# The window mask of the local attention, added by VectorE instead of TensorE

## The chip, the cores and the metric

One NeuronCore of a Trainium2 chip runs the whole program; seven other cores are idle. The metric is the time of one execution on the device, in microseconds, lower is better. Engines are named as in the profile: PE is TensorE, PEld its weight loads, DVE is VectorE, ACT is ScalarE, POOL is GpSimd, and SP issues the DMA transfers.

## The reference

The program is a two-layer block of a generator. Each layer normalises 1024 latent and 256 context tokens, projects them into four groups of heads (A: latent attention, B: global attention, C: attention within a window, with a sink, D: a state space scan), and projects the four results back. The change lies in group C. Cut to what matters, C computes for four heads of width 64:

```
def window_sink_attention(q, k, v, k_ctx, v_ctx, sink, scale):
    ...   # k_band: for each block of 128 queries the key blocks before, at and after it
    s_loc = jnp.einsum('bnqhgd,bnkhd->bnhgqk', qb, k_band).astype(jnp.float32) * scale
    s_ctx = jnp.einsum('bnqhgd,bkhd->bnhgqk', qb, k_ctx).astype(jnp.float32) * scale
    ...
    valid = (jnp.abs(k_pos - q_pos) <= WINDOW) & (k_pos >= 0) & (k_pos < n)
    s_loc = jnp.where(valid[None, :, None, None], s_loc, -jnp.inf)
    ...
    p = jax.nn.softmax(jnp.concatenate([s_ctx, s_loc, sink_col], axis=-1), axis=-1).astype(v.dtype)
    ...
```

WINDOW is 128. So a query block sees its own key block whole, a triangle of the block before and a triangle of the block after.

## The kernel before

Tokens are handled in tiles of 128. Attention runs over six pairs of heads per layer, in the order B, B, A, A, C, C. For each pair the queries come in groups (`gi`): 512 latent tokens, the other 512, and in the first layer the 256 context tokens. One group of one pair is a unit here. A unit has two interleaved activities:

- `main` computes the unit itself. For each key block and both heads it forms transposed scores in PSUM (tile `ps_st`, tag S2, three buffers), ACT writes their exponentials into `P` (L1224), two blocks later PE multiplies `P` with the values (L1231, tile `ps_acc`), and POOL or DVE adds `P` into running sums `ac` (L1240, L1246).
- Between its blocks `main` calls `pieces`: the steps of `maxima` for a later unit. Each step forms plain scores in PSUM (tile `ps_s`, tag MX, three buffers; L1143) and DVE takes the maximum of each row (L1147, tile `mp`), which later enters the exponent as one more row of the queries. In the last two units of a layer the pieces also split the output weights into high and low parts on DVE (`wo_hi` L1521, `wo_lo` L1522).

`mask_r` holds five blocks of 128 columns. The first three are the window mask: a triangle of 0 and -1e30, a block of zeros, the other triangle. In group C a score tile of 128, 256 or 384 columns gets the part of these three blocks that belongs to it (`mo` is its offset). Before the change it is added by PE: one more matmul with an identity as the weights accumulates the mask into the same PSUM tile, at L1145 for the maxima and at L1222 for the transposed scores.

The program is written as a sequence, and a scheduler orders the instructions of each engine and hands out buffers; each engine then runs its own list strictly in order. `tm` is a ring of eight buffers of 512 columns for short-lived tiles; `bg` is a ring of six buffers of 1024 columns that `P`, the raw weights `wo_raw` and the tiles `yh` and `yl` of the output projection share.

Of the kernel before, what the change touches and what calls it, by code (L numbers as in the profile page):

```python
# [9 lines left out]
F32 = mybir.dt.float32  # L10
F32R = mybir.dt.float32r
AF = mybir.ActivationFunctionType
ALU = mybir.AluOpType
# [4 lines left out]
P = 128  # L18
# [39 lines left out]
def hybrid_block(ctx, tc, x, ctxt, c_t, w_fm, w_tm, w_mod, b_gate, p_col, p_row, w_qu, w_kvu, w_out,  # L58
                 fnw, consts, rope_tm, rope_fm, out, dbg=None):
    nc = tc.nc  # L60
    DEPTH = w_fm.shape[0]
    cp = ctx.enter_context(tc.tile_pool(name="cp", bufs=1))
# [4 lines left out]
    mm = nc.tensor.matmul  # L67
# [44 lines left out]
    def small(shape, name, tag, bufs=2, dt=F32):  # L112
        return tp.tile(shape, dt, tag=tag, bufs=bufs, name=name)

    def ring(tag, bufs, cols):
        def f(shape=(P, cols), dt=F32, name=tag):
            return tp.tile(list(shape), dt, tag=tag, bufs=bufs, name=name)
        return f

    tm, ac, bg = ring("tm", 8, 512), ring("ac", 3, 1024), ring("bg", 6, 1024)  # L120
# [3 lines left out]
    def ps(tag, name=None):  # L124
        return pp.tile([P, 512], F32, tag=tag, bufs=PS_BUFS[tag], name=name or f"ps_{tag}")
# [6 lines left out]
    def f32(ap):  # L132
        return ap.bitcast(F32)
# [6 lines left out]
    def const(shape):  # L140

        n = int(np.prod(shape[1:]))
        v = con[:, con_at[0]:con_at[0] + n]
        con_at[0] += n
        assert con_at[0] <= CON_W
        return v if len(shape) == 2 else v.rearrange("p (a b) -> p a b", a=shape[1])
# [3 lines left out]
    ident, tri_u, tri_l, ones = [base[:, i * P:(i + 1) * P] for i in range(4)]  # L150
    rtm, cs = const([P, 8, 96]), const([P, 8, 32])
    mask_f = bg(name="mask_f")
    nc.sync.dma_start(out=mask_f[:, 0:5 * P], in_=consts[:, 4 * P:])
    mask_r = cp.tile([P, 6 * P], F32R, name="mask_r")
    nc.vector.tensor_copy(mask_r[:, 0:5 * P], mask_f[:, 0:5 * P])
    nc.vector.tensor_copy(mask_r[:, 5 * P:6 * P], ident)
    ident_r = mask_r[:, 5 * P:6 * P]
    st_r = [mask_r[:, 3 * P:4 * P], mask_r[:, 4 * P:5 * P]]
    mhalf = const([P, 16])
    nc.vector.memset(mhalf, -0.5)  # L160
    nc.vector.memset(cs, 0.0)
# [874 lines left out]
    def attention(L, res, need_ctx, y, late):  # L1036
# [90 lines left out]
        def maxima(op, gi):  # L1127
            lo, n = GROUPS[gi]
            nt = n // P
            br, kd = op["br"], op["kd"]  # L1130
            km = kd if br == 0 else P
            npc = 1 if gi == 0 else (3 if br < 2 else 2)
            st = {}

            def scored(h, parts, dst):

                qh = op["q"][h][0]
                kh = op["k"][h][0] if br == 0 else op["k"][0][0]
                p = ps("MX", name="ps_s")
                w = parts[0][2]  # L1140
                for u, (t, k0, w, mo) in enumerate(parts):
                    o = p[:, u * w:(u + 1) * w]
                    mm(o, lhsT=qh(lo + t * P, P, 0, km), rhs=kh(k0, w, 0, km), start=True, stop=mo is None)  # L1143
                    if mo is not None:
                        mm(o, lhsT=ident_r, rhs=mask_r[:, mo:mo + w], start=False, stop=True)  # L1145
                nu = len(parts)
                nc.vector.tensor_reduce(out=dst, in_=p[:, :nu * w].rearrange("p (u k) -> p u k", u=nu), axis=AX.X, op=ALU.max)  # L1147

            def begin():
                st["mp"] = small([P, 2, 4, 3], "mp", "mp", 2)  # L1150

            def ctx_part(h, t2):
                scored(h, [(t2 + u, 0, NCTX, None) for u in range(2)], st["mp"][:, h, t2:t2 + 2, 0])

            def lat_part(h, t, c):
                if br < 2:
                    scored(h, [(t, NCTX + c * 512, 512, None)], st["mp"][:, h, t, 1 + c:2 + c])
                else:
                    i = lo // P + t
                    j0, j1 = max(2, i - 1), min(NTILE - 1, i + 1)  # L1160
                    scored(h, [(t, j0 * P, (j1 - j0 + 1) * P, (j0 - i + 1) * P)], st["mp"][:, h, t, 1:2])

            def end():
                mt = small([P, 8], "mt", "mt", 2)
                mv = mt[:, 0:2 * nt].rearrange("p (h t) -> p h t", h=2)
                nc.vector.tensor_reduce(out=mv, in_=st["mp"][:, :, 0:nt, 0:npc], axis=AX.X, op=ALU.max)
                if br == 2:
                    p0 = op["pair"] * 2
                    nc.vector.tensor_tensor(out=mv, in0=mv, in1=sink8[:, p0:p0 + 2].unsqueeze(2).to_broadcast([P, 2, nt]), op=ALU.max)
                pm = ps("TR", name="ps_m")  # L1170
                nc.tensor.transpose(pm[0:2 * nt, 0:P], mt[:, :2 * nt], ident)
                ng = tm((8, P), F32R, name="ng")
                nc.scalar.activation(out=ng[0:2 * nt, :], in_=pm[0:2 * nt, 0:P], func=AF.Copy, scale=-1.0)
                for h in range(2):
                    nc.sync.dma_start(out=f32(op["q"][h][1](lo, n, kd, kd + 1)), in_=f32(ng[h * nt:(h + 1) * nt, :]))

            r = [begin]
            for h in range(2):
                r += [lambda h=h, t=t: ctx_part(h, t) for t in range(0, nt, 2)]
                if gi > 0:  # L1180
                    r += [lambda h=h, t=t, c=c: lat_part(h, t, c) for t in range(nt) for c in range(2 if br < 2 else 1)]
            return r + [end]
# [14 lines left out]
        def main(op, gi, pieces, tail):  # L1197
            lo, n = GROUPS[gi]
# [6 lines left out]
            def scores(bi):  # L1205
                kb, c0, w, mo = blocks[bi]
                k = lambda tok, rows: tok.tile(kb, 0, rows)
                pts = bg((P, 2, 512), name="P")
                for h in range(2):
                    st = ps("S2", name="ps_st")[:, :w]  # L1210
                    q0, q1 = op["q"][h]
                    q = lambda tok, rows: tok(lo + c0, w, 0, rows)
                    if br == 0:
                        k0, k1 = op["k"][h]
                        mm(st, lhsT=k(k0, 96), rhs=q(q0, 96), start=True, stop=False)  # L1215
                        mm(st, lhsT=k(k1, 96), rhs=q(q0, 96), start=False, stop=False)
                        mm(st, lhsT=k(k0, 97), rhs=q(q1, 97), start=False, stop=True)  # L1217
                    else:
                        k0, k1 = op["k"][0]
                        mm(st, lhsT=k(k0, 128), rhs=q(q0, 128), start=True, stop=False)  # L1220
                        if mo is not None:
                            mm(st, lhsT=ident_r, rhs=mask_r[:, mo:mo + w], start=False, stop=False)  # L1222
                        mm(st, lhsT=k(k1, 65), rhs=q(q1, 65), start=False, stop=True)  # L1223
                    nc.scalar.activation(out=pts[:, h, :w], in_=st, func=AF.Exp, scale=op["scale"])  # L1224
                return pts

# [30 lines left out]
            for bi in range(len(blocks)):  # L1257
                pts = scores(bi)
                batch.append((bi, pts))
                add(bi, pts)  # L1260
                if len(batch) == BATCH or bi == len(blocks) - 1:
                    for _ in range(2 if len(tail) > 3 else 1):
                        if tail:
                            tail.pop(0)()
                    flush_values()
                    todo.extend(batch)
                    batch = []
                want = min(total, -(-total * (bi + 1) // max(1, len(blocks) - LEAD)))
                while done < want:
                    pieces[done]()  # L1270
                    done += 1
            if br == 2:
                for h in range(2):
# [3 lines left out]
                                         scale=HEAD_SCALE, bias=pr[64:65, PR_SINK + hd:PR_SINK + hd + 1])  # L1277
                    nc.vector.tensor_tensor(out=sums[0][64:65, h, :n], in0=sums[0][64:65, h, :n], in1=es[64:65, :n], op=ALU.add)
            o = tm(name="o")
# [51 lines left out]
        for i, (br, pair) in enumerate(pairs):  # L1331
            op = ops[br, pair]
# [286 lines left out]
```

## Time and profile before

| | |
|---|---|
| time, median of 3 runs | 1849.13 us (1848.83 to 1856.71) |
| the profiled execution | 1844.81 us, its span 1843.0 us |
| busy share of the span | PE 95%, PEld 72%, DVE 61%, POOL 43%, ACT 40% |
| chain that ended last | PE 75%, DVE 11%, DMA 4%, issue 3%, POOL 3%, ACT 2% |

The span is what the profile covers, the time what the device reports for that execution. A busy share is a mean over stages with different limits. The chain is the sequence of waits followed back from the last instruction; an engine's share of it is the time during which that engine's work was what everything later waited for. In the first layer group C runs from about 787 us to 879 us of the span, in the second from about 1668 us to 1749 us; some of C's first maxima are already taken during the last unit of group A.

### The profile page before, as it was taken

How to read it: one execution, taken by the hardware profiler on the slowest of the kernel's cores; microseconds unless marked ns; L12 is line 12 of the kernel's file. 1: busy time of each engine (PE TensorE's matmuls, PEld its weight loads, DVE VectorE, ACT ScalarE, POOL GpSimd, SP SyncE). 2: the span in 40 equal slices, each digit the busy share in tenths (PEclk: the TensorE clock that was granted, in tenths of full speed). 3: DMA queues.
4: the chain of work that ended last, by engine and by line, in shares of the span. 5: the costliest groups of instructions: out<-in, count | busy, mean ns of one | idle time of the engine just before them, and what ended most of it. 6: DMA issues, size and time to landing. Idle time of an engine off the chain costs nothing.

```text
span 1843.0 us, 27921 instructions
## 1 busy us (share of the span) xinstructions
PE 1752.4 (95%) x9658; PEld 1329.2 (72%) x9658; DVE 1131.8 (61%) x2290; ACT 744.3 (40%) x2060; POOL 783.3 (43%) x735
## 2 busy tenths in 40 slices
PE   6999999999999999998999989999999999999898
PEld 4667888889975556565787768888998555566576
DVE  6867864373466655447546777753744766645953
ACT  5332433332224545556323333343332445455631
POOL 2322552132327766656224134531332576665522
PEclk9999999999999999999999989999999999999999
DMA  9474323255684332224411524231668623220521
GB/s 312 148 229 134 122 100 119 86 189 178 192 221 117 84 105 74 59 62 128 151 58 40 164 90 148 87 120 70 215 195 249 163 75 88 56 65 12 179 85 58
DMA packets 130397, 231.54 MB, mean 126 GB/s; under 512 B 13784, under 2 KB 74560, under 8 KB 130256
## 3 DMA queue, kind: packets, MB, share of 16 engines
q1 hardware_dynamic: 130256, 229.75, 40.2%
q8 instruction: 77, 1.26, 0.3%
q14 instruction: 64, 0.52, 0.1%
HBM read 161.15 MB, written 68.44 MB: 125 GB/s over the span
## 4 chain that ended last, share of the span: by engine, by line
PE 75%; DVE 11%; DMA 4%; issue 3%; POOL 3%; ACT 2%; SPq 0%; POOLq 0%; DVEq 0%; ACTq 0%
PE ps_acc L1231 10%; PE ps_fm L128 7%; PE ps_fm L130 7%; PE ps_fm L129 7%; PE ps_s L1143 6%; PE ps_o L129 3%; PE ps_o L130 3%; PE ps_o L128 3%; PE ps_st L1220 3%; PE ps_st L1223 3%; PE ps_tm L128 2%; PE ps_tm L130 2%; PE ps_tm L129 2%; PE ps_st L1215 2%; PE ps_st L1217 2%
## 5 line engine op out<-in xcount | busy, mean ns | idle before, releaser
L1246 POOL TENSOR_TENSOR ac<-ac,P 128x512 f32<-128x512 f32 (+3 forms) x248 | 310.8, 1274 | 134.8 <-ACT P L1224 114.5
L1147 DVE TENSOR_REDUCE mp<-ps_s 128x1 f32<-128x512 f32 (+3 forms) x428 | 260.7, 658 | 167.7 <-PE ps_s L1143 154.5
L1224 ACT ACTIVATE P<-ps_st 128x512 f32<-128x512 f32 (+3 forms) x456 | 238.0, 555 | 263.5 <-PE ps_st L1223 102.9
L128 PE MATMUL ps_fm<-hh,wfm_hi 128*128 128x512 f32 x576 | 234.3, 407 | 3.2 <-DVE kb L658 1.9
L130 PE MATMUL ps_fm<-hl,wfm_hi 128*128 128x512 f32 x576 | 231.3, 402 | 1.5 <-POOL hl L403 0.7
L129 PE MATMUL ps_fm<-hh,wfm_lo 128*128 128x512 f32 x576 | 229.9, 399 | 0.0
L128 PE MATMUL ps_tm<-wtm_hi,hh 128*128 128x256 f32 x512 | 146.5, 286 | 0.8 <-ACT va L870 0.6
L129 PE MATMUL ps_tm<-wtm_hi,hl 128*128 128x256 f32 x512 | 145.5, 284 | 0.0
L130 PE MATMUL ps_tm<-wtm_lo,hh 128*128 128x256 f32 x512 | 145.3, 284 | 0.0
L130 PEld LDWEIGHTS ps_fm<-hl,wfm_hi 128*128 128x128 f32 x576 | 109.2, 190 | 27.2 <-POOL hl L403 3.3
L128 PEld LDWEIGHTS ps_fm<-hh,wfm_hi 128*128 128x128 f32 x576 | 109.5, 190 | 26.5 <-ACT hf L399 3.3
L129 PEld LDWEIGHTS ps_fm<-hh,wfm_lo 128*128 128x128 f32 x576 | 109.6, 190 | 19.4 <-issue 0.8
L1240 POOL TENSOR_TENSOR ac<-P 128x1024 f32<-128x1024 f32 (+1 forms) x30 | 65.4, 2180 | 136.7 <-ACT P L1224 133.9
L128 PE MATMUL ps_o<-wo_hi,yh 128*128 128x512 f32 x288 | 113.3, 395 | 2.7 <-ACT yh L1373 2.7
L129 PE MATMUL ps_o<-wo_hi,yl 128*128 128x512 f32 x288 | 113.4, 394 | 0.5 <-DVE yl L1374 0.4
L130 PE MATMUL ps_o<-wo_lo,yh 128*128 128x512 f32 x288 | 112.9, 392 | 0.0
L1231 PE MATMUL ps_acc<-P,vt 128*64 128x512 f32 (+3 forms) x416 | 104.3, 542 | 0.0
L128 PEld LDWEIGHTS ps_tm<-wtm_hi,hh 128*128 128x128 f32 x512 | 98.1, 192 | 3.1 <-issue 1.6
L130 PEld LDWEIGHTS ps_tm<-wtm_lo,hh 128*128 128x128 f32 x512 | 98.2, 192 | 0.7 <-issue 0.4
L129 PEld LDWEIGHTS ps_tm<-wtm_hi,hl 128*128 128x128 f32 x512 | 98.2, 192 | 0.5
L1400 POOL TENSOR_TENSOR xres<-xres,dl 128x512 f32<-128x512 f32 x32 | 41.3, 1290 | 105.5 <-DVE dl L1399 105.5
L1246 DVE TENSOR_TENSOR ac<-ac,P 128x512 f32<-128x512 f32 (+3 forms) x88 | 64.8, 736 | 29.1 <-ACT P L1224 17.6
(345 smaller groups left out, 4150.4 us busy)
## 6 DMA issues: line engine op xcount, KB each, us to landing
wfm_raw<-in_w_fm_dram SPq DMA_DIRECT2D x36, 512.0 KB
wm<-in_w_mod_dram SPq DMA_DIRECT2D x64, 256.0 KB
d_q<-qkhl SPq DMA_DIRECT2D x18, 512.0 KB
wm<-in_w_mod_dram SPq DMA_DIRECT2D x16, 512.0 KB
d_gate<-th SPq DMA_DIRECT2D x32, 256.0 KB
wtm_raw<-in_w_tm_dram SPq DMA_DIRECT2D x16, 512.0 KB
qq<-d_q SPq DMA_DIRECT2D x32, 256.0 KB
wo_raw<-in_w_out_dram SPq DMA_DIRECT2D x16, 512.0 KB
```

The costliest lines, as they stand in the source:

```text
L128: mm(o, lhsT=lh, rhs=rh, start=first, stop=False)
L129: mm(o, lhsT=ll, rhs=rh, start=False, stop=False)
L130: return mm(o, lhsT=lh, rhs=rl, start=False, stop=last)
L1143: mm(o, lhsT=qh(lo + t * P, P, 0, km), rhs=kh(k0, w, 0, km), start=True, stop=mo is None)
L1147: nc.vector.tensor_reduce(out=dst, in_=p[:, :nu * w].rearrange("p (u k) -> p u k", u=nu), axis=AX.X, op=ALU.max)
L1220: mm(st, lhsT=k(k0, 128), rhs=q(q0, 128), start=True, stop=False)
L1223: mm(st, lhsT=k(k1, 65), rhs=q(q1, 65), start=False, stop=True)
L1224: nc.scalar.activation(out=pts[:, h, :w], in_=st, func=AF.Exp, scale=op["scale"])
L1231: mm(acc[h * 64:h * 64 + 64, c0:c0 + w], lhsT=op["v"].tile(kb)[:, v0:v0 + 64], rhs=pts[:, h, :w], start=(bi == 0), stop=(bi == len(blocks) ...
L1240: nc.gpsimd.tensor_tensor(out=s[:, :, :n], in0=sums[0][:, :, :n], in1=pts[:, :, :n], op=ALU.add)
L1246: eng.tensor_tensor(out=s[:, h, c0:c0 + w], in0=s[:, h, c0:c0 + w], in1=pts[:, h, :w], op=ALU.add)
L1400: (nc.vector if t == ts[-1] else nc.gpsimd).tensor_tensor(out=xt.t[:, js], in0=xt.t[:, js], in1=d, op=ALU.add)
```

## The change

The two masking matmuls are gone, and with them the identity in `mask_r`. In `maxima` one DVE instruction adds the mask to the scores and takes their maximum; it writes the sum to a buffer of the `tm` ring that nobody reads (`mjunk`). In `main` a DVE addition in place, in PSUM, stands between the matmuls and the exponential; it covers the two triangles only, not the zero block between them: 128 columns for a tile of 128 or 256 columns, two blocks of 128 for a tile of 384.

```
-    mask_r = cp.tile([P, 6 * P], F32R, name="mask_r")
-    nc.vector.tensor_copy(mask_r[:, 0:5 * P], mask_f[:, 0:5 * P])
-    nc.vector.tensor_copy(mask_r[:, 5 * P:6 * P], ident)
-    ident_r = mask_r[:, 5 * P:6 * P]
+    mask_r = cp.tile([P, 5 * P], F32R, name="mask_r")
+    nc.vector.tensor_copy(mask_r, mask_f[:, 0:5 * P])
     st_r = [mask_r[:, 3 * P:4 * P], mask_r[:, 4 * P:5 * P]]
+    win = mask_r.bitcast(F32)
...
-                    mm(o, lhsT=qh(lo + t * P, P, 0, km), rhs=kh(k0, w, 0, km), start=True, stop=mo is None)
+                    mm(o, lhsT=qh(lo + t * P, P, 0, km), rhs=kh(k0, w, 0, km), start=True, stop=True)
                     if mo is not None:
-                        mm(o, lhsT=ident_r, rhs=mask_r[:, mo:mo + w], start=False, stop=True)
+                        junk = tm(name="mjunk")
+                        nc.vector.tensor_tensor_reduce(out=junk[:, :w], in0=o, in1=win[:, mo:mo + w], scale=1.0, scalar=-3e38,
+                                                       op0=ALU.add, op1=ALU.max, accum_out=dst)
+                        return
...
                         mm(st, lhsT=k(k0, 128), rhs=q(q0, 128), start=True, stop=False)
-                        if mo is not None:
-                            mm(st, lhsT=ident_r, rhs=mask_r[:, mo:mo + w], start=False, stop=False)
                         mm(st, lhsT=k(k1, 65), rhs=q(q1, 65), start=False, stop=True)
+                    if mo is not None:
+                        b0, b1 = mo // P, (mo + w) // P - 1
+                        blocks_of = lambda v, b: v.rearrange("p (b c) -> p b c", c=P)[:, b, :]
+                        outer = slice(0 if b0 == 0 else 2 - b0, (2 if b1 == 2 else 0) - b0 + 1, 2)
+                        v = blocks_of(st, outer)
+                        nc.vector.tensor_tensor(out=v, in0=v, in1=blocks_of(win[:, 0:3 * P], slice(outer.start + b0, outer.stop + b0, 2)),
+                                                op=ALU.add)
                     nc.scalar.activation(out=pts[:, h, :w], in_=st, func=AF.Exp, scale=op["scale"])
```

The first place is DVE's list in the second layer, in the second unit of group C. Before, from the addition of a `P` of 128 columns to that of one of 384:

```order
L1246 TENSOR_TENSOR ac<-ac,P 128x128
L1147 TENSOR_REDUCE mp<-ps_s 128x1 x2
L1147 TENSOR_REDUCE mp<-ps_s 128x2
L1301 RECIPROCAL asum<-asum 128x8
L1147 TENSOR_REDUCE mp<-ps_s 128x2
L1147 TENSOR_REDUCE mp<-ps_s 128x1 x2
L1246 TENSOR_TENSOR ac<-ac,P 128x384
```

After the change (lines from 1143 on have moved by some numbers; ISA is the new combined instruction, and `mp 128x1` the second instruction that it becomes, which reads out its maximum):

```order
L1145 ISA mjunk,mp<-ps_s,mask_r 128x384
L1145 ISA mp 128x1
L1149 TENSOR_REDUCE mp<-ps_s 128x2
L1229 TENSOR_TENSOR ps_st<-ps_st,mask_r 128x128 x2
L1149 TENSOR_REDUCE mp<-ps_s 128x2
L1145 ISA mjunk,mp<-ps_s,mask_r 128x256
L1145 ISA mp 128x1
L1308 RECIPROCAL asum<-asum 128x8
L1145 ISA mjunk,mp<-ps_s,mask_r 128x384
L1145 ISA mp 128x1
L1229 TENSOR_TENSOR ps_st<-ps_st,mask_r 128x2x128 x2
```

The maxima keep their places, each masked one has become two instructions, and the additions for two score tiles at a time stand between them, behind whatever the list has ahead of them.

The second place is DVE's list in the last unit of group C in the second layer, where it also splits weights. Before:

```order
L1278 TENSOR_TENSOR ac<-ac,es 1x512 x2
L1521 CAST wo_hi<-wo_raw 128x512 x2
L1522 TENSOR_TENSOR wo_lo<-wo_raw,wo_hi 128x512 x2
L1246 TENSOR_TENSOR ac<-ac,P 128x128
L1521 CAST wo_hi<-wo_raw 128x512 x2
L1315 TENSOR_TENSOR y_16828<-rb,o 128x512
L1522 TENSOR_TENSOR wo_lo<-wo_raw,wo_hi 128x512 x2
L1301 RECIPROCAL asum<-asum 128x8
L1246 TENSOR_TENSOR ac<-ac,P 128x384
```

After the change, with the additions of the last unit's first three key blocks in the window:

```order
L1229 TENSOR_TENSOR ps_st<-ps_st,mask_r 128x128 x2
L1285 TENSOR_TENSOR ac<-ac,es 1x512 x2
L1528 CAST wo_hi<-wo_raw 128x512 x2
L1529 TENSOR_TENSOR wo_lo<-wo_raw,wo_hi 128x512
L1322 TENSOR_TENSOR y_16827<-rb,o 128x512
L1529 TENSOR_TENSOR wo_lo<-wo_raw,wo_hi 128x512
L1253 TENSOR_TENSOR ac<-ac,P 128x128
L1528 CAST wo_hi<-wo_raw 128x512 x2
L1529 TENSOR_TENSOR wo_lo<-wo_raw,wo_hi 128x512 x2
L1229 TENSOR_TENSOR ps_st<-ps_st,mask_r 128x128 x2
L1308 RECIPROCAL asum<-asum 128x8
L1229 TENSOR_TENSOR ps_st<-ps_st,mask_r 128x2x128 x3
```

The additions for the second key block stand behind all the weight splitting of this place, the additions for the third behind a reciprocal as well; the exponentials of these blocks can't begin before them.

## Rows read from the trace of the kernel before

**Rows 1.** The page: the span, and each engine's busy us, share and instructions.
```profile
span 1843.0 us, 27921 instructions
PE 1752.4 (95%) x9658; PEld 1329.2 (72%) x9658; DVE 1131.8 (61%) x2290; ACT 744.3 (40%) x2060; POOL 783.3 (43%) x735
```
**Rows 2.** Stretch; busy us (count) of PE, PEld, DVE, ACT, POOL; granted clock; DMA.
```profile
755.00:787.00 32.00, 32.00 (x153) 19.42 (x151) 10.81 (x20) 16.39 (x43) 21.39 (x16) 1.00 0.13 36
787.00:845.00 58.00, 54.46 (x305) 37.80 (x304) 35.52 (x73) 31.36 (x113) 28.12 (x26) 0.97 0.24 66
845.00:879.00 34.00, 25.70 (x147) 16.85 (x146) 26.57 (x46) 22.04 (x81) 21.79 (x16) 0.91 0.50 163
...
1668.00:1716.00 48.00, 47.65 (x263) 32.28 (x262) 31.11 (x56) 25.11 (x79) 26.92 (x25) 1.00 0.13 41
1716.00:1749.00 33.00, 27.51 (x143) 16.96 (x144) 29.62 (x47) 21.09 (x75) 17.26 (x15) 0.95 0.55 177
```
**Rows 3.** The chain by line in these five stretches, one row each, in order.
```profile
by line: PE ps_acc L1231 35.0%; PE ps_st L1217 16.2%; PE ps_st L1215 16.0%; PE ps_st L1216 16.0%; PE ps_s L1143 9.5%; PE ps_s L1145 4.1%; PE ps_sum L1295 2.7%; PE ps_m L1171 0.8%; PE ps_rt L1305 0.3%
...
by line: PE ps_acc L1231 25.2%; PE ps_s L1143 11.9%; PE ps_st L1220 11.8%; PE ps_st L1223 8.7%; PE ps_sum L1295 6.5%; PE ps_s L1145 4.3%; ACT junk L1298 3.9%; DVE mp L1147 3.9%; PE ps_st L1222 3.8%; ACT P L1224 3.3%; DVE y_cx L1315 3.1%; is
...
by line: issue 19.4%; DMA wo_raw<-in_w_out_dram 17.8%; DVE wo_lo L1522 7.9%; POOL ac L1246 7.1%; POOL ac L1240 6.9%; DVE wo_hi L1521 6.5%; PE ps_sum L1295 5.0%; PE ps_st L1220 5.0%; PE ps_st L1223 4.5%; PE ps_st L1222 4.3%; DVE ac L1278 3.6
...
by line: PE ps_acc L1231 28.6%; PE ps_st L1220 15.0%; PE ps_s L1143 14.9%; PE ps_st L1223 11.4%; PE ps_s L1145 6.7%; PE ps_st L1222 5.8%; issue 4.8%; PE ps_sum L1295 3.6%; ACT junk L1298 2.7%; ACT P L1224 2.3%; DVE ac L1246 1.2%; PE ps_m L1
...
by line: DMA wo_raw<-in_w_out_dram 15.2%; DVE wo_hi L1521 15.2%; issue 10.3%; ACT P L1224 9.0%; DVE wo_lo L1522 7.9%; PE ps_acc L1231 6.1%; PE ps_st L1220 5.4%; DVE ac L1278 5.3%; DVE y L1315 3.9%; PE ps_st L1223 3.4%; ACT wo_hi L289 3.2%; 
```
**Rows 4.** Groups by shape, the masking matmuls: busy us, mean ns, idle before.
```profile
L1145 PE MATMUL ps_s<-mask_r 128*128 128x384 f32 x48 | 16.3, 339 | 0.0
L1222 PE MATMUL ps_st<-mask_r 128*128 128x384 f32 x32 | 11.5, 358 | 0.0
L1222 PE MATMUL ps_st<-mask_r 128*128 128x256 f32 x32 | 9.2, 288 | 0.0
L1145 PE MATMUL ps_s<-mask_r 128*128 128x256 f32 x16 | 4.5, 280 | 0.0
L1222 PE MATMUL ps_st<-mask_r 128*128 128x128 f32 x16 | 4.4, 277 | 0.0
```
**Rows 5.** Line 1222 by stretch: busy us and count of its matmuls and weight loads.
```profile
787.00:845.00 58.00, 7.65 (x25) 4.85 (x26) 0.97 0.24 66
845.00:879.00 34.00, 5.23 (x15) 3.15 (x15) 0.91 0.50 163
...
1668.00:1716.00 48.00, 7.27 (x24) 4.59 (x25) 1.00 0.13 41
1716.00:1749.00 33.00, 4.96 (x16) 2.98 (x16) 0.95 0.55 177
```
**Rows 6.** Groups by shape on DVE, and ACT's reads of its accumulator.
```profile
L1147 DVE TENSOR_REDUCE mp<-ps_s 128x1 f32<-128x384 f32 x48 | 24.9, 549 | 12.4 <-PE ps_s L1145 12.4
L1399 DVE TENSOR_TENSOR dl<-ps_o,gb 128x512 f32<-128x512 f32 x36 | 24.8, 689 | 72.7 <-PE ps_o L130 68.3 <-DMA d_rs<-rrow 2.2 <-PE ps_sum L1295 2.0
L1246 DVE TENSOR_TENSOR ac<-ac,P 128x128 f32<-128x128 f32 x8 | 4.5, 561 | 8.3 <-POOL ac L1246 2.9 <-ACT P L1224 2.7 <-POOL ac L1240 2.7
L1315 DVE TENSOR_TENSOR yd_cx<-rb,o 128x256 f32<-128x256 f32 x2 | 0.8, 420 | 2.5 <-DMA rb<-d_rs 2.5
L1166 DVE TENSOR_REDUCE mt<-mp 128x4 f32<-128x4 f32 x6 | 0.9, 154 | 0.1
...
L1298 ACT ACTIVATION_READ_ACCUMULATOR junk<-ps_sum 128x1 f32 x216 | 48.7, 226 | 0.1
```
**Rows 7.** DVE's timeline in the second layer: start us, us, instruction.
```profile
1692.17 2.29 DVE L1315 TENSOR_TENSOR y<-rb,o 128x512 f32<-128x512 f32 x1
...
1727.43 3.88 DVE L1278 TENSOR_TENSOR ac<-ac,es 1x512 f32<-1x512 f32 x2 [2.44 <-ACT es L1276]
```
**Rows 8.** Busy us, columns as in rows 2, of 5 us of the first layer.
```profile
815.00:820.00 5.00, 5.00 (x21) 2.62 (x20) 2.36 (x6) 2.29 (x16) 1.98 (x4) 0.68 0.00 0
```

## The prediction

> **What bounds the kernel now.** I read the page first, for the shares: PE is busy 95% of a span of 1843.0 us, DVE 61% [rows 1]. That invites moving work from PE to DVE, but it is a mean over stages, so the next views are the busy times and the chain of waits in the stretches that hold group C [rows 2, 3]. The reader is to see three kinds of stretch. At the end of group A (755 to 787) PE is busy for all 32 us, the chain consists of PE alone, and DVE works 10.8 us: PE sets the pace. In the early part of C (787 to 845, 1668 to 1716) PE is still most of the chain, but DVE already works 35.5 of 58 and 31.1 of 48 us. In the late part (845 to 879, 1716 to 1749) the chain goes through weight transfers and weight splitting; DVE works 26.6 of 34 and 29.6 of 33 us, and PE's own lines have small shares. So the change takes work from PE in all of them, and gives DVE more where DVE has least to spare.
>
> **What is removed.** 64 matmuls in the maxima and 80 in the scores [rows 4]. Their durations overlap, so the sum of them is no saving; what counts is their part of the chain [rows 3]. End of A: 4.1% of 32 us is 1.3, and the second layer's end of A, whose 28 us read alike, is taken as 1.3 too. Early C in the first layer: 4.3% and 3.8% of 58 us, 4.7. Late C: 4.3% of 34 us, 1.5. Early C in the second layer: 6.7% and 5.8% of 48 us, 6.0. Late C in the second: neither line is among those listed, so each has under 3.2% of 33 us; I take nothing. Sum 14.8 us. This is the most that taking the matmuls away can give. The removed copy of the identity is one short DVE instruction at the start; I count nothing.
>
> **What is added in the scores.** 80 DVE additions, 48 over 128 columns (16 tiles of 128 and 32 of 256) and 32 over two blocks of 128 [rows 4]. No row shows DVE writing to PSUM. The nearest rows are an addition of a PSUM tile and an SBUF tile over 512 columns, 689 ns, and an undisturbed one over 256 columns, 420 ns [rows 6]: 1.05 ns per column, so 286 ns for 128 and 420 ns for 256. That is 48 x 0.286 + 32 x 0.420 = 27.2 us, 0.34 us each. From below, none can be shorter than the shortest DVE instruction of that group, 154 ns: 12.3 us. From above I take the 561 ns that the addition of 128 columns to the running sums needs on average, and 134 ns more for the wider ones: 49.2 us. I take 27.2, because the 689 ns row has the same two kinds of operands.
>
> The 561 ns against 286 have a reason that matters here: that addition has both inputs in SBUF, and POOL works beside it. On ports, the Trainium skill (SBUF — State Buffer, section "SBUF: two separate sides") says that DVE and POOL lock a shared pair of ports for a whole instruction, on DVE's side only for instructions with two SBUF inputs or in a two-port mode. By that rule the new additions, with one input in PSUM, are free of it, and the sum stays at 27.2; were they not, it would be 49.2. The trace speaks for the rule: the addition with a PSUM input keeps 689 ns over 36 instances.
>
> **What is added in the maxima.** The combined instruction stands where the maximum stood. 689 less 128 x 1.05 is 555 ns for 384 columns, and the maximum alone takes 549 [rows 6]: nothing, if it goes at that speed. No row shows it; at half speed it would be 0.5 us more, 32 us over 64. I take nothing. The read of the maximum is one more DVE instruction, between 154 ns and the 226 ns that ACT needs for such a read [rows 6]; I take 160 ns, since it is a DVE instruction on one column: 10.2 us over 64, 3.8 us for the 24 that fall into each early part of C (8 per layer fall into A's end, where DVE has 21 us free).
>
> The combined instruction also waits for a buffer of the ring that `rb`, `o` and `ng` use, the last one read by DMAs. DVE's whole list would stand behind such a wait, the maxima and the masks of the scores; with eight buffers the earlier reader is usually long done. I cost it at nothing, and at up to 2 us in the range.
>
> **The sum by stretch**, DVE after the change against PE after it [rows 2, 5]:
> - End of A, both layers: DVE has room. The whole gain, -2.6 us.
> - Early C, first layer: DVE 35.5 + 25 x 0.34 + 3.8 = 47.8 us; the chain without masks 53.3. There is room on paper, but a score tile now waits for PE, DVE and ACT in turn, with three buffers, and the DVE list puts maxima between the additions. Half the gain, -2.4 (from -4.7 to +3).
> - Early C, second layer: DVE 31.1 + 24 x 0.34 + 3.8 = 43.1; the chain without masks 42.0. Two engines that both need 42 to 43 us and wait for each other can't make it in 43; 47, so -1 (from -5 to +4).
> - Late C, first layer: DVE 26.6 + 15 x 0.34 = 31.7 of 32.5. DVE idles 7 us of 34 today because it waits for DMA and ACT, and the additions lengthen that same round, so I count 5.1 of added time less 1.5 saved, and half a us of it as hidden: +3 (from -1.5 to +6).
> - Late C, second layer: DVE 29.6 + 16 x 0.34 = 35.0 us of work in a stretch of 33. At least +2 whatever the order. The additions for the second and third key block come behind the splitting of weights and behind two additions that took 3.88 us in POOL's shadow [rows 7], so some idle time stays: +4 (from +2 to +7).
> - The clock. Behind a gap of PE in the first layer 5 us ran at a granted 0.68 [rows 8], between the two levels of 1.2 and 2.4 GHz; that cost 5 x 0.32 = 1.6 us. PE has fewer matmuls and longer gaps now. One more such fall: +1.6 (from 0 to +5). The Trainium skill (TensorE: Matmul & The Clock Gate, section "Why this matters for your kernels") also asks for matmuls without idle gaps between them, and this change makes gaps; the trace agrees, with that 0.68.
>
> Together -2.6 - 2.4 - 1 + 3 + 4 + 1.6 = +2.6 us. The ends, all together: -11.8 and +24.4, with 2 us for the ring. The profiled execution is 1844.81 us, 1.8 us around its span; it would become 1847.4. The median of the runs shown is 1849.13, 4.3 above it, so the forecast of a median is 1852 us.
>
> **The rivals.** *DVE hides it.* The additions fit beside PE and nothing waits for them: the 14.8 us are gained, less the 2 us that late C of the second layer can't avoid: 1836 us. For it: the busy shares of 95% and 61%, and that exponentials are used two key blocks later. Against it: 43.1 us of DVE work in a 48 us stretch. *DVE's list becomes the bound.* One DVE instruction that POOL holds up takes 2 to 4 us [rows 7]; when additions stand behind it, the three score buffers fill, PE stops, and the time shows at full length. There are eight units with masks; if one additional wait of 2 us per unit goes through, the forecast rises by 16 us, to 1868. It decides from 0.8 us per unit on, 6.6 us in all, since the forecast already has 2.6. Put otherwise: of 80 additions at 0.34 us, 44 on the chain eat the gain, 71 make the kernel slower by 0.5%. For it: the order in both places shown. Against it: PE is most of the chain in early C. *The combined instruction runs at half speed.* Then 24 x 0.5 = 12 us of DVE work come to each early C, 55 us against 48 and 60 against 58: about 9 us and 5 us over what I have, 1866 us. *The scheduler's new order* shifts transfers of weights either way; it is within the bounds of late C.
>
> **How the numbers follow.** A measurement of this kernel tells about 0.5% from no change, 9.2 us. Forecast, within that: 0.48. DVE hides it, faster by more: 0.18. DVE's list or a slow combined instruction, slower by more: 0.34, of which 0.08 is the latter. The range for 8 in 10 runs from 1840 to 1868 us; the likeliest case's own is 1841 to 1858.
>
> **What would show it.** In the changed profile: 144 matmuls and their weight loads gone; 80 additions near 0.29 and 0.42 us; the combined instruction near 0.55 us for 384 columns and its read near 0.16; the end of A 1.3 us shorter per layer; DVE busy above 90% from early C on, and exponentials that wait for DVE where they waited for PE; the late part of C in the second layer longer by 2 us or more. The prediction is wrong if additions take over 0.5 us, if the combined instruction takes 1 us, or if the early parts of C shrink by all of their 11 us or grow by more than 5.

## The result, and the profile after

The changed kernel takes 1865.13 us (median of 4, 1863.12 to 1867.86) against 1850.53 us for the kernel before beside it: a ratio of 1.0078, 95% interval 1.0056 to 1.0099. It is slower by 0.8%, 14.6 us, inside the range on record, 13 us above the point. The profiled execution took 1863.24 us. Its page answers to [rows 1]:

```profile
span 1861.4 us, 27812 instructions
...
PE 1769.3 (95%) x9514; PEld 1319.1 (71%) x9514; DVE 1151.9 (62%) x2433; ACT 742.8 (40%) x2060; POOL 782.7 (42%) x735
```

144 matmuls are gone, and PE is busy for 17 us more. That is the first thing to see: with fewer matmuls, each one on average takes longer. The windows say where. This is the changed kernel from group C's first score to a score in the middle of pair 1, and from there to the first product of the output projection, in both layers (columns as in [rows 2]):

```profile
783.88:845.62 61.74, 56.20 (x248) 31.55 (x246) 37.40 (x102) 31.31 (x113) 28.30 (x25) 0.92 0.20 58
845.62:888.04 42.42, 33.08 (x136) 16.95 (x135) 32.98 (x75) 20.97 (x80) 18.70 (x16) 0.88 0.41 128
1679.76:1728.41 48.65, 46.10 (x216) 25.52 (x214) 34.33 (x94) 22.89 (x76) 24.31 (x22) 1.00 0.08 25
1728.41:1762.57 34.16, 28.18 (x110) 14.41 (x110) 30.81 (x64) 19.91 (x70) 18.31 (x17) 0.80 0.48 161
```

And this the kernel before, cut at the same instructions, which [rows 2] cut at round times:

```profile
787.06:844.23 57.17, 53.63 (x301) 37.03 (x299) 34.74 (x69) 31.36 (x113) 28.09 (x25) 0.97 0.24 66
844.23:876.87 32.64, 24.66 (x145) 16.52 (x144) 25.27 (x44) 20.72 (x79) 21.79 (x16) 0.94 0.46 149
1668.36:1715.84 47.48, 47.12 (x263) 32.12 (x261) 30.95 (x56) 25.11 (x79) 26.40 (x25) 1.00 0.13 41
1715.84:1744.68 28.84, 23.86 (x129) 14.45 (x128) 25.81 (x40) 17.17 (x62) 16.45 (x15) 0.94 0.49 152
```

The four stretches grew by 4.6, 9.8, 1.2 and 5.3 us, 20.8 together. The spans of these two executions differ by 18.4; the ends of group A give back 1.3 each. (The profiled execution of the kernel before took 1844.81 us, less than its median, so the two differ by more than the medians' 14.6.) Read the granted clock beside the lengths: 0.92, 0.88, 1.00 and 0.80 where it was 0.97, 0.94, 1.00 and 0.94. Length times what is missing to 1 is the clock lost: 16.9 us after, 5.4 before.

One of these falls, in windows of 2 us of the changed kernel:

```profile
852.00:854.00 2.00, 1.71 (x8) 1.07 (x9) 1.53 (x7) 0.00 (x0) 0.71 (x1) 1.00 0.00 0
854.00:856.00 2.00, 0.31 (x2) 0.10 (x1) 2.00 (x8) 0.00 (x0) 0.00 (x0) 1.00 0.00 0
856.00:858.00 2.00, 0.98 (x6) 0.55 (x6) 2.00 (x8) 1.39 (x9) 0.52 (x1) 1.00 0.00 0
858.00:860.00 2.00, 0.79 (x1) 0.29 (x1) 2.00 (x7) 0.41 (x4) 2.00 (x1) 0.54 0.01 3
860.00:862.00 2.00, 1.93 (x6) 1.54 (x7) 0.69 (x4) 1.52 (x5) 0.97 (x2) 0.50 0.01 2
...
866.00:868.00 2.00, 2.00 (x6) 0.74 (x6) 1.87 (x4) 1.95 (x4) 1.49 (x3) 0.50 0.00 0
868.00:870.00 2.00, 2.00 (x7) 0.42 (x5) 2.00 (x2) 0.06 (x1) 1.56 (x1) 0.90 0.01 4
```

From 854 to 860 DVE is busy without a break and PE works 2.1 of 6 us; then PE works again, at a granted 0.50, 1.2 GHz, for some 10 us. What DVE did there, and what PE waited for, from the timelines of DVE and of PE:

```profile
847.92 2.09 DVE L1528 CAST wo_hi<-wo_raw 128x512 fp32r<-128x512 f32 x2
849.93 1.28 DVE L1529 TENSOR_TENSOR wo_lo<-wo_raw,wo_hi 128x512 fp32r<-128x512 f32 x2
851.14 0.29 DVE L1229 TENSOR_TENSOR ps_st<-ps_st,mask_r 128x128 f32<-128x128 f32 x1
851.34 0.41 DVE L1145 CUSTOM_DVE_ANT_0 mjunk<-ps_s,mask_r 128x256 f32<-128x256 f32 x1
...
854.69 0.68 DVE L1149 TENSOR_REDUCE mp<-ps_s 128x2 f32<-128x512 f32 x1
855.29 0.68 DVE L1322 TENSOR_TENSOR y<-rb,o 128x512 f32<-128x512 f32 x1
855.89 0.16 DVE L1171 TENSOR_TENSOR mt<-mt,con 128x8 f32<-128x8 f32 x1
...
856.77 1.28 DVE L1529 TENSOR_TENSOR wo_lo<-wo_raw,wo_hi 128x512 fp32r<-128x512 f32 x2
```
```profile
856.19 0.65 PE L1173 MATMUL ps_m<-con,mt 128*8 128x128 f32 x2 [1.89 <-DVE mt L1168]
...
858.53 0.79 PE L1223 MATMUL ps_st<-ql,kk_cx 65*128 65x512 f32 x1 [1.25 <-DMA ql<-ng]
```

DVE's list splits weights (`wo_hi`, `wo_lo`), then masks a score, then takes the last five masked maxima. The next unit's scores need those maxima: PE waits for `mt`, then for the transfer that brings them into `ql`. In the kernel before the same maxima were done by 844, ahead of the splitting. Between 847.92 and 859.85 DVE's list has a single addition, 0.29 us long: so what fills it ahead of the maxima is the splitting. e1 below, which has no addition at all, falls in the same place, to 0.50 from 860 to 868.

DVE's durations in the changed kernel, by shape, answer to [rows 6]:

```profile
L1145 DVE CUSTOM_DVE_ANT_0 mjunk<-ps_s,mask_r 128x384 f32<-128x384 f32 x48 | 25.3, 551 | 7.0 <-PE ps_s L1142 7.0
...
L1229 DVE TENSOR_TENSOR ps_st<-ps_st,mask_r 128x128 f32<-128x128 f32 x48 | 13.1, 290 | 18.7 <-ACT P L1231 9.3 <-PE ps_st L1223 9.2
L1229 DVE TENSOR_TENSOR ps_st<-ps_st,mask_r 128x256 f32<-128x256 f32 x32 | 12.7, 423 | 9.3 <-issue 4.9 <-PE ps_st L1223 4.4
...
L1145 DVE DVE_READ_ACCUMULATOR2_ANT mp<- 128x1 f32 x64 | 5.2, 81 | 0.0
```

ACT's waits over the whole span (us in total, times, longest us) show a new one, exponentials that wait for an addition. The first line is the kernel before, the others are the changed one:

```profile
ACT P L1224 <- PE ps_st L1223: 102.9, 78, 4.8
...
ACT P L1231 <- PE ps_st L1223: 71.7, 57, 4.1
...
ACT P L1231 <- DVE ps_st L1229: 40.9, 25, 5.6
```

The new wait looks like the culprit. But most of it stands where a wait for PE stood before: the two lines after come to 112.6 us, against 102.9 before. And e9 below has a loss of the same size with 6 us of such waits.

### The profile page after: what moved, and what is told of

Same layout as the page of the kernel before. It is cut to its first block, busy times and chain, and to the rows that moved or that the text cites. A ratio compares the mean times of both kernels' runs of the same rounds, so it can differ in the third digit from the quotient of the medians.

```text
span 1861.4 us, 27812 instructions
## 1 busy us (share of the span) xinstructions
PE 1769.3 (95%) x9514; PEld 1319.1 (71%) x9514; DVE 1151.9 (62%) x2433; ACT 742.8 (40%) x2060; POOL 782.7 (42%) x735
## 5 line engine op out<-in xcount | busy, mean ns | idle before, releaser
L1253 POOL TENSOR_TENSOR ac<-ac,P 128x512 f32<-128x512 f32 (+3 forms) x248 | 304.3, 1247 | 152.5 <-ACT P L1231 134.1
L1149 DVE TENSOR_REDUCE mp<-ps_s 128x1 f32<-128x512 f32 (+1 forms) x364 | 231.3, 682 | 143.4 <-PE ps_s L1142 142.9
L128 PEld LDWEIGHTS ps_fm<-hh,wfm_hi 128*128 128x128 f32 x576 | 110.5, 192 | 25.9 <-issue 3.0
L1238 PE MATMUL ps_acc<-P,vt 128*64 128x512 f32 (+3 forms) x416 | 117.8, 543 | 1.6 <-ACT P L1231 1.6
L1222 PE MATMUL ps_st<-qq,kk 128*128 128x512 f32 (+3 forms) x208 | 80.7, 390 | 1.2 <-ACT P L1231 1.0
```

What stands on the lines that cost most here:

```text
L128: mm(o, lhsT=lh, rhs=rh, start=first, stop=False)
L1238: mm(acc[h * 64:h * 64 + 64, c0:c0 + w], lhsT=op["v"].tile(kb)[:, v0:v0 + 64], rhs=pts[:, h, :w], start=(bi == 0), stop=(bi == len(blocks) ...
L1253: eng.tensor_tensor(out=s[:, h, c0:c0 + w], in0=s[:, h, c0:c0 + w], in1=pts[:, h, :w], op=ALU.add)
```

## The experiments

Each was timed beside the kernel before, so kernels of different rounds are best compared by their ratios; the intervals reach some 3 to 5 us to either side. "Clock lost" is the span times what is missing to 1 in its mean granted clock, the median over the executions. The kernel before ran 77 times beside them: it lost 16.6 to 35.3 us of clock, and its time followed, 1840.9 to 1857.4 us, by a straight line of 0.78 us per us lost (correlation 0.86). The last column takes 0.78 of the clock lost off the time, so that kernels can be compared as if at one clock; that the same line holds for the other kernels is assumed.

| kernel | time, us | ratio to before (95%) | clock lost | time less 0.78 of it |
|---|---|---|---|---|
| before | 1849.3 | 1 | 25.9 | 1829.1 |
| changed | 1865.1 | 1.0078 (1.0056 to 1.0099) | 39.2 | 1834.5 |
| e1_maxima_only | 1855.6 | 1.0032 (1.0016 to 1.0048) | 30.6 | 1831.7 |
| e2_scores_only | 1867.0 | 1.0090 (1.0063 to 1.0117) | 32.6 | 1841.6 |
| e3_no_score_mask | 1840.8 | 0.9944 (0.9924 to 0.9963) | 29.4 | 1817.9 |
| e4_after_no_split | 1867.5 | 1.0104 (1.0084 to 1.0124) | 41.0 | 1835.5 |
| e5_before_no_split | 1863.2 | 1.0086 (1.0066 to 1.0106) | 32.6 | 1837.8 |
| e6_after_hi_on_act | 1857.9 | 1.0055 (1.0038 to 1.0073) | 37.2 | 1828.9 |
| e7_after_score_mm_twice | 1866.6 | 1.0097 (1.0077 to 1.0117) | 38.3 | 1836.7 |
| e8_before_hi_on_act | 1843.4 | 0.9975 (0.9959 to 0.9991) | 20.3 | 1827.6 |
| e9_add_after_exp | 1863.9 | 1.0071 (1.0043 to 1.0098) | 40.0 | 1832.7 |
| e10_pair0_on_dve | 1855.0 | 1.0031 (1.0012 to 1.0050) | 32.4 | 1829.7 |
| e11_trimmed_and_hi_on_act | 1848.4 | 0.9991 (0.9975 to 1.0008) | 22.2 | 1831.1 |
| e12_split_after_maxima | 1849.5 | 1.0007 (0.9991 to 1.0022) | 26.8 | 1828.6 |

### Which half of the change costs: e1, e2, e3

The theory was that the additions cost the time (Q), against the combined instruction (M) and the new order (S).

e1 keeps the scores' masking matmuls and takes the new maxima:

```
                     if mo is not None:
-                        mm(o, lhsT=ident_r, rhs=mask_r[:, mo:mo + w], start=False, stop=True)
+                        junk = tm(name="mjunk")
+                        nc.vector.tensor_tensor_reduce(out=junk[:, :w], in0=o, in1=win[:, mo:mo + w], scale=1.0, scalar=-3e38,
+                                                       op0=ALU.add, op1=ALU.max, accum_out=dst)
+                        return
```

> Only the maxima are masked on DVE; the scores keep their masking matmuls. Theory Q (the additions stand in DVE's in-order list, ahead of the exponentials, and cost the time): the 64 matmuls of the maxima leave the chain, 8 us at most, less up to 5 us for 64 reads of 0.081 us, so 3 to 8 us faster than before, 1842 to 1848, and pair 1 of group C as long as before in both layers. Rival M (the combined instruction, its ring buffer and its read hold DVE up): slower than before by 8 us or more, 1858 and up. Rival S (any change gives the scheduler another order, and the order is what was lost): anything from 1850 to 1865, with pair 1 longer.

Slower by 0.3%, 5.4 us, instead of faster: Q missed. e2 is the other half, the additions with the maxima's masking matmuls kept:

```
-                        if mo is not None:
-                            mm(st, lhsT=ident_r, rhs=mask_r[:, mo:mo + w], start=False, stop=False)
...
+                        nc.vector.tensor_tensor(out=v, in0=v, in1=blocks_of(win[:, 0:3 * P], slice(outer.start + b0, outer.stop + b0, 2)),
+                                                op=ALU.add)
```

> Only the scores are masked on DVE; the maxima keep their masking matmuls. Q: the whole loss and none of the maxima's gain, 1866 to 1873, with pair 1 of group C longer by 12 us in the first layer and 6 us in the second. M: as before or faster by the 6 us that the scores' matmuls had on the chain, 1843 to 1852. S: 1850 to 1868.

1867.0 us, as Q had it: the additions alone cost as much as the whole change. Pair 1 grew by 8.3 us in the first layer, where Q had 12, and by 6.8 in the second, where it had 6 (the lengths are in the table under e12). e3 leaves the additions out of the changed kernel; its scores stay unmasked:

```
+    nc.vector.memset(win[:, 0:3 * P], 0.0)
...
-                    if mo is not None:
...
-                        nc.vector.tensor_tensor(out=v, in0=v, in1=blocks_of(win[:, 0:3 * P], slice(outer.start + b0, outer.stop + b0, 2)),
-                                                op=ALU.add)
```

> The changed kernel without its 80 additions: the scores are not masked at all, and the combined instruction adds zeros where the mask was, at the same size. What it is faster by than the changed kernel is what the additions cost with all that they bring. Q: the full gain of the removed matmuls, up to 14.8 us, less the reads: 1836 to 1844, 20 us or more under the changed kernel. M: still slower than before, 1855 and up. S: between 1845 and 1865.

1840.8 us: taking 144 matmuls away is worth some 9 to 10 us, as Q had it, and the 80 additions cost 24.3 us, close to the 25.8 us that they are busy for in the changed kernel, though e10 will show that this is no price per addition. M falls. That the maxima alone lose 5 us was open.

### Load, wait, or missing matmuls: e4 to e7, e9

e4 and e5 split no weights during group C, in the changed kernel and in the one before:

```
-N_LATE = 3
+N_LATE = 0
```

> The changed kernel with no weights split during group C; all of them are split in the output projection, as far as they don't fit there already. To be read against e5_before_no_split, the kernel before with the same edit. Theory K (the additions come on top of bursts of DVE work in pair 1, PE runs dry behind them and its clock falls): without the splitting the two differ by under 5 us, and pair 1 of the changed kernel is under 52 us long in the first layer (62.5 with the splitting) with under 4 us of clock lost. Rival H (the additions cost what they cost because each is one more step between score and exponential, splitting or not): they differ by 10 us or more.

> The kernel before with no weights split during group C: the base for e4_after_no_split. Against the kernel before itself, K and H both expect a few us more, 1850 to 1875, since the splitting now stands in the output projection; that cost is the same for both kernels.

They differ by 4.3 us (3.3 by the ratios) where the kernels with splitting differ by 14.6: K's bound of 5 held, H's of 10 didn't. Moving the splitting made the kernel before 13.9 us slower, the changed one 2.4, which is within the noise. The lengths that K named can't be read: the output projection now waits for the splitting, so its first product is no mark for the end of pair 1. From pair 0's last unit, a short one, to pair 1's last the changed kernel takes 45.0 us without splitting, 55.3 with it; the kernel before takes 39.0 and 42.0. So the two are 6.0 us apart there without splitting, 13.3 with it: it makes the larger part of the difference, not all. K also expected the clock back, and the whole execution still loses 41.0 us of it. In the last column e4 even lies 2.3 us below e5, so by that measure nothing but clock is left between them.

e6 only moves the casts to ACT:

```
-                    nc.vector.tensor_copy(st[1].t[:, js], st[0][:, js])
+                    nc.scalar.copy(st[1].t[:, js], st[0][:, js])
```

> The changed kernel with the high parts of the weights in group C made by ACT instead of DVE: 16 casts of 0.42 to 0.77 us leave DVE's list in the first layer and as many as fit in the second. K: a burst of DVE work is shorter, fewer falls of the clock, 1850 to 1858. H: as the changed kernel, 1861 to 1867.

1857.9 us, just inside K's range: 7.2 less than the changed kernel by the medians, 4.3 by the ratios, whose intervals overlap. The clock lost stays at 37.2, so little of the gain was in the clock. e7 gives PE 80 of its 144 matmuls back:

```
+                        if mo is not None:
+                            mm(st, lhsT=k(k0, 128), rhs=q(q0, 128), start=True, stop=True)
                         mm(st, lhsT=k(k0, 128), rhs=q(q0, 128), start=True, stop=False)
```

> The changed kernel with the first matmul of each masked score tile done twice, the second time over the first, so that PE has about the work of before. Rival F (the clock falls because PE has fewer matmuls): the clock lost goes back to about 26 us per execution and the time to 1850 to 1856. K and H: PE waits for DVE as before, and the matmuls come on top: 1863 to 1873, with 35 us or more of clock lost.

1866.6 us with 38.3 us of clock lost: F falls: with these matmuls back the clock stays as low. They don't fill the gaps.

e9 gives DVE its additions behind the exponentials instead of ahead of them; its scores stay unmasked, as in e3:

```
                     nc.scalar.activation(out=pts[:, h, :w], in_=st, func=AF.Exp, scale=op["scale"])
+                    if mo is not None:
+                        c = P if w < 3 * P else 2 * P
+                        junk = tm(name="sjunk")
+                        nc.vector.tensor_tensor(out=junk[:, :c], in0=pts[:, h, :c], in1=win[:, 0:c], op=ALU.add)
```

> As e3_no_score_mask (scores not masked), but with 80 DVE additions of the same sizes one step later: each reads the finished exponentials and writes to a buffer that nobody reads, so DVE has the additions to do and no exponential waits for them. If the load on DVE's list costs the time (L): near the changed kernel, 1858 to 1868. If it is that each exponential has to wait for an addition (H): near e3_no_score_mask, 1840 to 1848.

1863.9 us, 23.1 above e3 and 1.2 below the changed kernel: as load (L) had it. Its additions by shape on DVE:

```profile
L1229 DVE TENSOR_TENSOR sjunk<-P,mask_r 128x128 f32<-128x128 f32 x48 | 16.9, 392 | 0.6 <-ACT junk L1303 0.5
...
L1229 DVE TENSOR_TENSOR sjunk<-P,mask_r 128x256 f32<-128x256 f32 x32 | 15.2, 517 | 0.0
```

With both inputs in SBUF they are busy for 32.1 us, 6.3 more than in the changed kernel. Nor are they free of waits: in e9's trace three later exponentials waited 6.2 us in all for such an addition, and two other ACT instructions as much. So the run shows that a loss of that size doesn't need each exponential to wait for its own addition, not that such a wait costs nothing.

### Where it costs: e10, and the splitting by itself: e8, e11

e10 masks pair 0's scores on DVE and pair 1's on PE:

```
+                        if mo is not None and op["pair"] == 1:
+                            mm(st, lhsT=ident_r, rhs=mask_r[:, mo:mo + w], start=False, stop=False)
...
-                    if mo is not None:
+                    if mo is not None and op["pair"] == 0:
```

> The changed kernel with the scores of pair 1 masked by PE as before, those of pair 0 by DVE, the maxima all on DVE. K (the additions cost where the weights are split): 1850 to 1857, as e1_maxima_only (1855.6). H (each addition costs alike): halfway between e1_maxima_only and the changed kernel, 1859 to 1862.

1855.0 us, as e1 without any addition: pair 0's 40 additions, in place of 40 matmuls, change nothing that can be measured, to within some 5 us. Pair 1's 40, where the weights are split, cost 10.1 us by the medians, 8.7 by the ratios. H falls. e8 is the control for e6, the same edit on the kernel before:

> The kernel before with the high parts of the weights in group C made by ACT: the control for e6_after_hi_on_act, which gained 7 us over the changed kernel. If the additions are what fills DVE's list in pair 1 (K), the kernel before gains little by the same relief, 0 to 3 us: 1846 to 1850. If the splitting costs that much whatever the masks (rival G), it gains 5 to 8 us as well: 1841 to 1845.

Faster than before, by 6.1 us of the medians, 4.6 us by the ratio: nearer to G than to K. The casts on DVE cost some 4 to 7 us with or without the change, so e6 says nothing of the additions alone. The two gains aren't alike: e8 loses 20.3 us of clock where the kernel before loses 25.9, and in the last column 1.5 us of its gain are left, while e6 keeps 5.6 of its own. e11 shortens the scores' wide masking matmuls as well:

```
+                            if w == 3 * P:
+                                two = lambda v: v.rearrange("p (b c) -> p b c", c=P)[:, 0:3:2, :]
+                                mm(two(st), lhsT=ident_r, rhs=two(mask_r[:, 0:3 * P]), start=False, stop=False)
```

> A candidate: the kernel before, with the masking matmul of a score tile of 384 columns over its two triangles only (256 columns), and the high parts of the weights on ACT. The 32 shorter matmuls give 0.05 us each at most, 1.7 us together; with what e8_before_hi_on_act gives, 1841 to 1849 and faster than both kernels if the relief counts, 1848 to 1852 if it doesn't.

No difference from before can be told (0.9975 to 1.0008). Its interval overlaps with e8's, and what it lacks against e8 isn't explained. Of the kernels that mask their scores, e8 alone beats both, the one before by a quarter of a per cent.

### Why the maxima alone are slower: e12

e12 is e1 with the splitting held behind the last maximum of its unit:

```
+                last_max[0] = nc.cur_bb.bb.instructions[-1]
...
+                    with tc.issue_after(last_max[0]):
                         nc.vector.tensor_copy(st[1].t[:, js], st[0][:, js])
```

> As e1_maxima_only (maxima masked on DVE, scores by PE), with one more rule of order on DVE's list: the splitting of weights is issued behind the last maximum of the unit. In e1_maxima_only, in the changed kernel and in every other kernel here with the combined instruction, the first layer's pair 1 has two weight halves split ahead of five of the maxima; in the kernel before and in e2_scores_only all maxima come first. Theory S (that order is what made e1_maxima_only 5 us slower than before, although it has 64 matmuls less): 1842 to 1850, and the last maximum of that unit ends by 845 us. Rival C (the combined instruction and its read cost it themselves): as e1_maxima_only, 1853 to 1858.

1849.5 us, the time of the kernel before: S had it, and the new order accounts for e1's loss, 4.6 us by the ratios, though the two intervals still overlap a little. C falls. DVE's timeline of e1 in the first layer's pair 1:

```profile
846.34 2.35 DVE L1526 TENSOR_TENSOR wo_lo<-wo_raw,wo_hi 128x512 fp32r<-128x512 f32 x2
848.61 0.67 DVE L1525 CAST wo_hi<-wo_raw 128x512 fp32r<-128x512 f32 x1
849.21 0.41 DVE L1147 CUSTOM_DVE_ANT_0 mjunk<-ps_s,mask_r 128x256 f32<-128x256 f32 x1
...
851.26 0.42 DVE L1147 CUSTOM_DVE_ANT_0 mjunk<-ps_s,mask_r 128x256 f32<-128x256 f32 x1 [0.20 <-PE ps_s L1144]
```

and of e12:

```profile
847.86 0.42 DVE L1148 CUSTOM_DVE_ANT_0 mjunk<-ps_s,mask_r 128x256 f32<-128x256 f32 x1 [0.20 <-PE ps_s L1145]
...
850.91 0.42 DVE L1528 CAST wo_hi<-wo_raw 128x512 fp32r<-128x512 f32 x1
```

The last masked maximum ends at 848.3 instead of 851.7, not by 845 as expected, and it was enough, though e12 still falls there, to 0.50 from 856 to 860. But e12 has 64 matmuls less than before and is no faster.

The profiles tell where each half costs. These are lengths in us of one execution each, from pair 0's last unit to the first product of the output projection in the first layer, and from pair 1's first score to that product in the second; in brackets, the clock lost in them:

| kernel | first layer | second layer |
|---|---|---|
| before | 49.3 (2.0) | 40.3 (1.7) |
| changed | 62.5 (8.5) | 46.5 (6.8) |
| e1_maxima_only | 62.6 (11.1) | 40.7 (3.4) |
| e2_scores_only | 57.6 (7.1) | 47.1 (5.1) |
| e10_pair0_on_dve | 55.4 (5.1) | 40.7 (0.5) |
| e12_split_after_maxima | 52.0 (3.4) | 42.0 (5.1) |

In the second layer only the kernels with additions in pair 1 are clearly longer, by 6 to 7 us. In the first layer e1, which has no addition, is as long as the changed kernel, and e12 takes most of that back; e2, with additions and the old order, is longer by 8.3. So by these lengths the order costs in the first layer alone, the additions in both. The parts don't add up, and e10, with e1's work in pair 1, is 7 us shorter than e1, 6 of them clock, so a single length is good to some us only.

## Why the prediction was right, and where it was off

Slower by over 0.5%, which it gave 0.34, came true, and the time lies inside the range of 1840 to 1868 us. The likelier case, within 0.5% (0.48), and its own range to 1858 didn't come true: the forecast itself, +2.6 us, was too low, and it is the width of the range that holds the result. Of its five stretches the ends of group A came out as forecast, two within their bounds, two beyond them.

**The term that was furthest off is the clock.** It had one more fall, +1.6 us, from 0 to 5. The executions of the changed kernel lose 39.2 us of clock against 25.9; at 0.78 us each that is 10.4 us of the 15.8 between the medians of the table. The other terms had +1.0 together and came to 5.4. The pattern was there before the change, a gap of PE (2.95 of 5 us busy from 810 to 815) and then the clock of 0.68 in [rows 8], and the prediction counted one more such gap where several came. The Trainium skill (TensorE: Matmul & The Clock Gate, section "Why this matters for your kernels") asks for matmuls without idle gaps; the trace agrees, with the 0.50 from 860 to 868 behind a PE that worked 2.1 of 6 us. The share isn't the same in every kernel: e2, as slow as the changed one, has 5.2 of its 17.7 us from the clock. That the clock is a cause of the time, and not only a sign of the same gaps, rests on that straight line over 77 executions of one program and on these windows; no run here changed the clock alone.

**The prices were right.** Additions 290 and 423 ns (286 and 420 forecast), the combined instruction 551 for 384 columns (555); only its read, 81, was half of what was taken (160). The rule on ports of the Trainium skill (SBUF — State Buffer, section "SBUF: two separate sides") fits the runs: additions of the same sizes took 290 and 423 ns with an input in PSUM, 392 and 517 in e9 with both in SBUF, where the shortest took 274 and the longest 1364. (e9's also write to SBUF instead of PSUM; no run separates the two.)

**By stretch.** End of A: from the token sums to C's first score 24.13 us became 22.85, and 20.63 became 19.34 in the second layer: 1.3 each, as forecast. The first layer's early C, forecast -2.4, grew by 4.6 and late C, forecast +3, by 9.8: both beyond their bounds. Less 0.78 of the clock lost they grew by 2.1 and 7.3, so late C's bound of +6 fails without the clock too: what it lacked, by e1 and e12, is the order of splitting and maxima. The second layer's early C grew by 1.2 (-1 forecast) and late C by 5.3 (+4), within bounds; of the latter 4.0 is clock by the same measure. One sign of being wrong that the prediction gave came true: the early parts, read as a sum like its 11 us, grew by 5.7 us, over its 5.

**The gain was there.** At most 14.8 us, the prediction said; without additions 9.4 were seen, 11.2 at one clock.

**The rivals.** "DVE's list becomes the bound" gave 1868, 3 us off, but its mechanism, additions behind a held-up instruction so that exponentials wait, isn't needed for the loss by e9. Its price was misread too: the 3.88 us of [rows 7] are two additions, so one took about 1.9. And it holds in one place only; in pair 0 "DVE hides it" was right. "The scheduler's new order" was put within the bounds of late C; that was too narrow, since by itself it cost e1's 5 us. "The combined instruction runs at half speed" came nearest in number, 1866, and was wrong: 551 ns is the speed of the plain maximum (549). The ring's buffer never delayed the changed kernel's combined instruction: all 7.0 us that DVE idled before it were waits for PE.

**Of what should show it**, exponentials do wait for DVE, 25 times; but DVE isn't above 90% from early C on: it is busy 61, 78, 71 and 90% of the four stretches.

**Open.** How the additions' cost in pair 1 divides between load and wait; how much of the loss the clock causes; why the changed kernel's clock stays low without the splitting (e4); whether e12's rule would help the changed kernel, which wasn't tried.

## What to carry to other kernels

Ask of an engine with spare time whether it is spare in the stretch where the work lands: 40 additions in place of 40 matmuls cost nothing that could be measured in one pair of heads, and 40 like them cost 9 to 10 us in the next, where the same list also split weights. Count the gaps that a change can open on TensorE, and look at the granted clock behind each, not only at its own length. And when a change alters an instruction's form, look at where its neighbours went in the list: a rule of order for the weight splitting gave e1's 5 us back.

## What the runs showed of the hardware

The kernel before varied by 16 us between executions of one program, and the clock lost went along with it. Taking the clock lost off brought e10 within 1 us of the kernel before; it left e2 12.5 us and e5 8.7 us above it. DVE's read of an accumulated maximum takes 81 ns, about half of its shortest instruction in [rows 6], and in the changed kernel's timeline the next combined instruction starts together with it (both at 852.16 us): the combined instruction costs hardly more than the plain maximum.
